# A hybrid encoder layer: level tiles in two sets, inverse blocks in four transfers, rotary halves exchanged by ScalarE

## The chip, the cores and the metric

The kernel runs on one core of a Trainium2 chip. The metric is the device time of one execution in microseconds (us), the median of several runs. Times inside an execution are read from a profile of one run, counted from the start of its span.

## What is computed

One layer of a bidirectional encoder over 1024 tokens of width 1024, in float32. Cut to what matters here:

```python
h = rms_norm(x, g_mix_pre)
proj = h @ w_in                      # attention q, k, v; delta q, k, v; gate; decay and beta
aq, ak = rope(aq), rope(ak)          # rotary positions, head width 64, halves of 32
attn_o = window_attention(aq, ak, av, sink)      # +-128 tokens, 8 heads on 2 key heads
dn_o = gated_deltanet(dqkv, gate, alpha, beta)   # 4 heads, two directions, chunked
x = x + rms_norm(concat(attn_o, dn_o) @ w_out)
x = x + rms_norm(cross_attention(rms_norm(x), rms_norm(mem)))
x = x + rms_norm(swiglu(rms_norm(x)))

def rope(x):                         # x1, x2 are the two halves of 32 of a head
    return concat([x1 * cos - x2 * sin, x2 * cos + x1 * sin])
# deltanet, per chunk: solve (I + strictly lower part) u = rhs, then a scan over the chunks
```

The reference works in chunks of 64 tokens. The kernel works in chunks of 128, for both directions, and inverts the triangular matrix of each chunk.

## The kernel before

The sequence lies in eight chunks of 128 tokens (NT = 8), feature rows on the partitions. Products are made in split precision: an operand is split into a high and a low part, and three products are summed (a projection of 128 columns is 24 matmuls of 128x512 for each half of 512 tokens, line 261). Weights come in by `load_w` (raw tile, then `whi` on ScalarE and `wlo` on VectorE). All transfers are issued by the SyncE queue, SP. The Tile framework puts the instructions of each engine in an order by priority (the order of the program) and a timing model, and adds the waits; each engine then works through its own list in that order. A tile's tag with `bufs=n` has n buffers; a new tile of that tag waits until one of them is free.

Three lists written by hand set the program's order. `ORDER_1` runs the projections of the delta heads (D), their preparation (P) and the base inverses of a pair of heads (B). `ORDER_2` is the part around the change:

```python
ORDER_2 = "L0 L1 G0 G1 A4 V A0 A1 L2 L3 W W W A2 A3 G2 G3 W".split()
```

L is `levels` of a delta head, G a gate projection, A an attention projection with rotary positions (A4 is the keys), V the value projection, W a pair of attention windows. `ORDER_3` then runs the scan of the delta heads (`s01`), which needs the result `d_pz` of all four heads, mixed with the remaining windows and with the cross-attention's keys and values.

**Levels.** `base_inverse` inverts all 32x32 diagonal blocks of a pair of heads by a chain of small VectorE products and stores them in DRAM (`d_inv`, lines 541 to 544). `levels(h)` builds from them the inverse of each 128x128 triangle, by two block products. It has large tiles `D5`, `D6`, `Z0`, `Z1` (128 x 8 x 128), zero off the diagonal blocks, in which the 32x32 blocks are placed at their diagonal position. Before the change there is one set of these (`wide_sets`, line 717), cleared once by POOL (line 719). The blocks come by twenty transfers for each head: for each of the four block rows `q` one to `m5`, one each into the diagonal place in `D5`, `D6`, `Z0`, `Z1` (`fetch`, line 551; each 32 x 8 x 32 numbers in runs of 128 bytes). A head is worked on in two halves of four chunks each (`part`), which alternate at each `yield`: load `Ul` (572), transpose (576), masks to `L5` and `L6` (577, 578), product with `L5` and `D5` (585, 591), small copies of the result `z5` to `D6`, `Z` and `mov6` (596 to 605), product with `L6` and `D6`, then `Z` to `d_pz` (610). `L5`, `L6` and `Ul` have two buffers each.

**Attention projection.** `attn_proj` multiplies each half of the product, in an accumulator bank of the pool `pg` (three banks), by the sine into `sn` and by the cosine into `rop`; four transfers for each half exchange blocks of 32 partitions from `sn` to `rot` (line 734); VectorE adds `rot` (735), ScalarE and VectorE split the sum into `qhi` and `qlo`, and both are stored. `sinT` carries the sign of the source row. `sn` shares its tag `rot` with `vT` of the value projection (line 745). Windows load the stored queries (`qs`, line 625).

Of the kernel before, what the change touches and what calls it, by code (L numbers as in the profile page):

```python
# [10 lines left out]
F32 = mybir.dt.float32  # L11
F32R = mybir.dt.float32r
I32 = mybir.dt.int32
AF = mybir.ActivationFunctionType
ALU = mybir.AluOpType
# [4 lines left out]
P = 128  # L20
# [12 lines left out]

ORDER_1 = "D0 P0 D1 P1 D2 B0 P2 D3 P3 B1".split()
ORDER_2 = "L0 L1 G0 G1 A4 V A0 A1 L2 L3 W W W A2 A3 G2 G3 W".split()
ORDER_3 = ("M " + "s01 W K " * 5 + "s01 K " * 3 + "s01 V V").split()
# [8 lines left out]
def host_constants():  # L47
    i = np.arange(P)
    blk = i // 32
    a, b = i[:, None], i[None, :]  # L50
    ba, bb = blk[:, None], blk[None, :]
    tri = {
        "ident": a == b,
        "mU": a < b,
        "mL": a > b,
        "mUi": a <= b,
        "mLi": a >= b,
        "m5": (ba // 2 == bb // 2) & (ba != bb),
        "m6": ba // 2 != bb // 2,
        "ones": a + b >= 0,  # L60
    }
    out = np.zeros((P, _NCONST), np.float32)
    for n, m in tri.items():
        out[:, _AT[n]:_AT[n] + P] = m

    out[:, _AT["band0"]:_AT["band0"] + P] = np.where(b >= a, 0.0, NEG)
    out[:, _AT["band2"]:_AT["band2"] + P] = np.where(b <= a, 0.0, NEG)
    half = np.arange(32, dtype=np.float32)
    inv = np.power(np.float32(10000.0), -half / np.float32(32)).astype(np.float32)
    out[:, _ROPE_AT] = inv[i % 32]  # L70
    out[:, _ROPE_AT + 1] = np.where(i % 64 < 32, 1.0, -1.0)
    return out


# [1 line left out]
def tile_hybrid_block(  # L76
# [469 lines left out]
    def levels(h):  # L546

        g, hh = h // 2, h % 2

        def fetch(dst, q, i, d):  # L550
            nc.sync.dma_start(dst, d_inv[g][i][d, hh, :, q].rearrange("c r s -> r c s"))

        m5 = tl_.tile([P, NT, 32], F32, tag="m5", name="m5", bufs=1)
        D5a, D6a, *Za = wide_sets[0]
        for q in range(4):
            r = slice(32 * q, 32 * q + 32)
            fetch(m5[r], q, 1, 1 - q % 2)
            fetch(D5a[r, :, r], q, 0, q % 2)
            fetch(D6a[r, :, r], q, 0, q // 2)
            for d in range(2):  # L560
                fetch(Za[d][r, :, r], q, 1, d)

        def part(b):
            c4 = slice(4 * b, 4 * b + 4)

            def wide(name):
                return tl_.tile([P, 4, P], F32, tag=name, name=name, bufs=2)

            L5, L6 = wide("L5"), wide("L6")
            D5, D6, Z = D5a[:, c4], D6a[:, c4], [z[:, c4] for z in Za]  # L570
            Ul = wide("Ul")
            nc.sync.dma_start(Ul, d_u[g][hh, c4].rearrange("c p n -> p c n"))
            yield
            p_ = small().rearrange("p (c n) -> p c n", c=4)
            for j in range(4):
                nc.tensor.transpose(p_[:, j, :], Ul[:, j, :], ident)
            nc.vector.tensor_tensor(L5, p_, bc(cm["m5"], 1, (P, 4, P)), ALU.mult)
            nc.vector.tensor_tensor(L6, p_, bc(cm["m6"], 1, (P, 4, P)), ALU.mult)

            def pair(lt, mv, dd, w):  # L580

                yield
                p_ = small()[:, 0:4 * w].rearrange("p (c n) -> p c n", c=4)
                for c in range(4):
                    nc.tensor.matmul(p_[:, c, :], lt[:, c, :], mv[:, c, :], start=True, stop=True)
                bs = tl_.tile([P, 4, 64], F32, tag="bs", name="bs", bufs=2)[:, :, 0:w]
                nc.scalar.copy(bs, p_)
                yield
                p_ = small()[:, 0:4 * w].rearrange("p (c n) -> p c n", c=4)
                for c in range(4):  # L590
                    nc.tensor.matmul(p_[:, c, :], dd[:, c, :], bs[:, c, :], start=True, stop=True)
                return p_

            p_ = yield from pair(L5, m5[:, c4, :], D5, 32)
            z5 = tl_.tile([P, 4, 32], F32, tag="z5", name="z5", bufs=2)
            nc.scalar.mul(z5, p_, -1.0)
            nc.vector.transpose(D6[32:64, :, 0:32], z5[0:32])
            nc.vector.transpose(D6[64:96, :, 96:128], z5[96:128])
            nc.vector.tensor_copy(Z[1][32:64, :, 0:32], z5[32:64])
            nc.vector.tensor_copy(Z[0][64:96, :, 96:128], z5[64:96])  # L600
            mov6 = tl_.tile([P, 4, 64], F32, tag="mov6", name="mov6", bufs=2)
            nc.scalar.copy(mov6[0:64], Z[1][0:64, :, 0:64])
            nc.vector.tensor_copy(mov6[64:128], Z[0][64:128, :, 64:128])
            nc.scalar.copy(Z[0][0:32, :, 32:64], z5[0:32])
            nc.scalar.copy(Z[1][96:128, :, 64:96], z5[96:128])
            p_ = yield from pair(L6, mov6, D6, 64)
            nc.scalar.mul(Z[0][0:64, :, 64:128], p_[0:64], -1.0)
            nc.vector.tensor_scalar(Z[1][64:128, :, 0:64], p_[64:128], -1.0, None, ALU.mult)
            for d in range(2):
                nc.sync.dma_start(d_pz[g][d][c4, :, hh, 1].rearrange("c p n -> p c n"), Z[d])  # L610

        together([part(b) for b in range(2)])
# [60 lines left out]
    keys, vhl = {}, None  # L673

    def window_keys(g):
        keys[g] = tw.tile([P, S], F32R, tag="khi", name="khi"), tw.tile([P, S], F32R, tag="klo", name="klo", bufs=1)
        for kk, src in zip(keys[g], d_k):
            for r in range(2):
                nc.sync.dma_start(f32(kk[64 * r:64 * r + 64]), src[64 * g:64 * g + 64, :])
# [32 lines left out]
    ps = pgs.enter_context(pool("psl", 2, space=PSUM))  # L712
    tw = p12.enter_context(pool("tw", 2))
    tw.tile([P, 384], F32, tag="sc", name="sc", bufs=8)
    vhl = tw.tile([P, NT + 1, 2, 2, 64], F32R, tag="vhl", name="vhl", bufs=1)[:, 0:NT]
    tl_ = p1.enter_context(pool("tl", 2))
    wide_sets = [[tl_.tile([P, NT, P], F32, tag=f"{n}{i}", name=n, bufs=1) for n in ("D5", "D6", "Z0", "Z1")] for i in range(1)]
    for t in wide_sets[0]:
        nc.gpsimd.memset(t, 0.0)

    def attn_proj(ct):
        pp = proj(w_in[:, ct * P:(ct + 1) * P])
        dst = [t[ct * P:(ct + 1) * P, :] if ct < 4 else t for t in (d_q if ct < 4 else d_k)]
        for hf in range(2):
            sl = slice(hf * HALF, (hf + 1) * HALF)
            rop = trp.tile([P, HALF], F32, tag="rop", name="rop")
            sn = trp.tile([P, HALF], F32, tag="rot", name="sn")
            rot = trp.tile([P, HALF], F32, tag="rot2", name="rot2")
            nc.vector.tensor_tensor(sn, pp[hf], sinT[:, sl], ALU.mult)
            nc.vector.tensor_tensor(rop, pp[hf], cosT[:, sl], ALU.mult)  # L730

            for q in range(4):
                o = 32 * (q ^ 1)
                nc.sync.dma_start(rot[32 * q:32 * q + 32], sn[o:o + 32])
            nc.vector.tensor_tensor(rop, rop, rot, ALU.add)
            hl = [trp.tile([P, HALF], F32R, tag=t, name=t) for t in ("qhi", "qlo")]
            split(*hl, rop)
            for t, o in zip(hl, dst):
                nc.sync.dma_start(o[:, sl], f32(t))
# [785 lines left out]
```

## Time and profile before

| | us |
|---|---|
| median of three runs | 1551.69 |
| lowest and highest | 1547.02, 1553.25 |
| profiled execution | 1555.78 |
| its span, first to last instruction | 1554.1 |
| mean granted TensorE clock | 0.983 |
| stretch of the levels and attention projections | about 221 to 373 |

The profiled execution is one run; its span is shorter than its time by 1.7 us, which lie around the instructions. In the rows, PE is TensorE (PEld its weight loads), DVE VectorE, ACT ScalarE, POOL GpSimd, SPq the queue of SyncE. The view by stretches gives the busy time of each engine in a part of the span, its number of instructions in brackets, the granted TensorE clock as a share of full speed, the mean busy share of the 16 DMA engines and their GB/s. A row of a tile's or a line's view gives, in ns, the shortest, the median and the longest of its instructions, then the start of the first and the last. A row of the waits gives who waited for whom, in us in all, how often, and the longest. A row of the chain gives the start, the length and what it was.

### The profile page before, as it was taken

What the parts mean: (1) busy time and instruction counts of PE and PEld (TensorE: products, weight loads), DVE (VectorE), ACT (ScalarE), POOL (GpSimd) and SP (SyncE); (2) the same over time, 40 slices, a digit from 0 to 9 for tenths busy, and PEclk for the clock granted to TensorE, in tenths of its full rate; (3) what the DMA queues carried; (4) which work ended last, traced back from release to release, by engine and by line L of the source; (5) the groups of instructions that cost most, each with busy time, mean ns of one, the idle gap of its engine ahead of it and who ended that gap; (6) DMA issues with size and microseconds to landing.
All of it is one profiled execution on the core that took longest, in us unless ns stands there. A gap on an engine that the chain in (4) does not pass through costs nothing.

```text
span 1554.1 us, 20931 instructions
## 1 busy us (share of the span) xinstructions
PE 1497.3 (96%) x7451; PEld 1258.1 (81%) x7451; DVE 1055.9 (68%) x1750; ACT 719.6 (46%) x1380; POOL 308.3 (20%) x305
## 2 busy tenths in 40 slices
PE   6999999898899999999999999999999999999998
PEld 5888888787899877888888777888888888888786
DVE  6777898766898766443447367776867554687665
ACT  6666552246556755454335574332323332454532
POOL 2000110000003201163102221433533333000021
PEclk9999999997999999999999999999999999999999
DMA  6244456867987584354213264344434334863354
GB/s 211 69 136 128 125 157 160 217 179 245 319 278 247 164 283 165 119 190 148 82 55 123 85 200 141 111 135 129 134 122 132 102 102 141 288 193 102 108 175 165
DMA packets 267366, 247.16 MB, mean 159 GB/s; under 512 B 39016, under 2 KB 204797, under 8 KB 267261
## 3 DMA queue, kind: packets, MB, share of 16 engines
q1 hardware_dynamic: 267261, 245.82, 50.7%
q8 instruction: 59, 0.97, 0.3%
q14 instruction: 46, 0.38, 0.1%
HBM read 173.65 MB, written 69.50 MB: 156 GB/s over the span
## 4 chain that ended last, share of the span: by engine, by line
PE 80%; DVE 6%; DMA 6%; ACT 3%; issue 2%; SPq 2%; POOL 0%; DVEq 0%; POOLq 0%; ACTq 0%
PE pg L261 13%; PE pmg L1016 10%; PE pD L1196 8%; PE pE L1196 8%; PE pA L1196 6%; PE pcq L261 6%; PE pdX L1386 6%; PE pdA L1386 4%; PE pB L1196 4%; PE psc L785 2%; PE pdX L1479 2%; PE pdD L1386 2%; DMA wraw<-in_w_ckv_dram 2%; PE pcs L1102 1%; PE pco L1128 1%
## 5 line engine op out<-in xcount | busy, mean ns | idle before, releaser
L102 ACT CAST whi<-wraw 128x1024 fp32r<-128x1024 f32 x108 | 113.5, 1051 | 173.3 <-PE pg L261 36.0
L103 DVE TENSOR_TENSOR wlo<-wraw,whi 128x1024 fp32r<-128x1024 f32 x78 | 95.5, 1225 | 77.7 <-ACT whi L102 75.0
L261 PE MATMUL pg<-hhi,whi 128*128 128x512 f32 x352 | 140.8, 401 | 0.2 <-DVE rop L730 0.2
L261 PE MATMUL pg<-hhi,wlo 128*128 128x512 f32 x352 | 140.2, 399 | 0.0
L261 PE MATMUL pg<-hlo,whi 128*128 128x512 f32 x352 | 139.9, 398 | 0.0
L1016 PE MATMUL pmg<-whi,b 128*128 128x512 f32 x384 | 118.4, 394 | 0.4 <-ACT b L102 0.4
L1196 PE MATMUL pA<-s,whi 128*128 128x512 f32 x352 | 109.5, 392 | 1.4 <-ACT m L1213 1.4
L103 POOL TENSOR_TENSOR wlo<-wraw,whi 128x1024 fp32r<-128x1024 f32 x30 | 73.8, 2460 | 143.3 <-ACT whi L102 143.2
L1016 PEld LDWEIGHTS pmg<-whi,b 128*128 128x128 f32 x384 | 71.3, 188 | 15.2 <-ACT b L102 1.3
L261 PEld LDWEIGHTS pg<-hhi,whi 128*128 128x128 f32 x352 | 67.3, 192 | 14.0 <-DVE rop L730 0.7
L261 PEld LDWEIGHTS pg<-hlo,whi 128*128 128x128 f32 x352 | 67.2, 191 | 13.2
L261 PEld LDWEIGHTS pg<-hhi,wlo 128*128 128x128 f32 x352 | 67.2, 191 | 13.1
L1196 PEld LDWEIGHTS pA<-s,whi 128*128 128x128 f32 x352 | 65.3, 188 | 15.2 <-ACT m L1213 2.0
L1386 PE MATMUL pdX<-dhl,whi 128*128 128x512 f32 x264 | 76.1, 390 | 1.5 <-DVE zv L1441 0.8
L1016 PE MATMUL pmg<-wlo,b 128*128 128x512 f32 x192 | 71.5, 392 | 0.0
L1196 PE MATMUL pA<-s,wlo 128*128 128x512 f32 x176 | 68.7, 392 | 1.1 <-DVE wlo L103 1.1
L102 ACT CAST whi<-araw 128x1024 fp32r<-128x1024 f32 (+1 forms) x36 | 35.4, 984 | 69.9 <-PE pdX L1386 27.6
L1273 POOL TENSOR_TENSOR act<-act,up 128x512 f32<-128x512 f32 x33 | 50.1, 1519 | 89.1 <-DVE up L1272 53.1
L103 DVE TENSOR_TENSOR wlo<-araw,whi 128x1024 fp32r<-128x1024 f32 (+1 forms) x36 | 40.8, 1133 | 38.4 <-ACT whi L102 38.3
L286 DVE SCALAR_TENSOR_TENSOR acc<-cp,cols,acc 128x1024 f32<-128x1024 f32 x48 | 61.5, 1282 | 1.5 <-ACT acc L284 0.8
L1386 PEld LDWEIGHTS pdX<-dhl,whi 128*128 128x128 f32 x264 | 49.3, 188 | 12.8 <-issue 1.1
L1246 DVE TENSOR_TENSOR sr<-sr,wraw 128x512 f32<-128x512 f32 x22 | 37.8, 1716 | 29.8 <-POOL sr L1245 29.8
(409 smaller groups left out, 3976.7 us busy)
## 6 DMA issues: line engine op xcount, KB each, us to landing
wraw<-in_w_gate_up_dram SPq DMA_DIRECT2D x52, 512.0 KB, 4.0
kv<-d_kv SPq DMA_DIRECT2D x32, 512.0 KB, 6.6
wraw<-in_w_in_dram SPq DMA_DIRECT2D x22, 512.0 KB, 5.5
b<-in_w_down_dram SPq DMA_DIRECT2D x20, 512.0 KB, 6.8
araw<-d_as SPq DMA_DIRECT2D x20, 512.0 KB, 3.8
pz<-d_pz SPq DMA_DIRECT2D x32, 256.0 KB, 6.8
wraw<-in_w_ckv_dram SPq DMA_DIRECT2D x16, 512.0 KB, 6.4
wraw<-in_w_out_dram SPq DMA_DIRECT2D x16, 512.0 KB, 4.3
```

Of the source, the lines that this page charges most:

```text
L102: nc.scalar.copy(hi, src)
L103: (eng or nc.vector).tensor_tensor(lo, src, f32(hi), ALU.subtract)
L261: nc.tensor.matmul(p_, w[:, k, :], ah[a][:, k, :], start=(k == 0 and i == 0), stop=(k == nk - 1 and i == 2))
L286: nc.vector.scalar_tensor_tensor(acc, cp[:, t:t + S], taps[t], acc, ALU.mult, ALU.add)
L785: nc.tensor.matmul(out[:, d, h, :], lt[:, d, h, :], rt[:, d, h, :], start=True, stop=True)
L1016: nc.tensor.matmul(pp[t], act[a][:, k, tt], w_[:, kk, :], start=(k == 0 and i == 0), stop=(k == KT - 1 and i == 2))
L1102: nc.tensor.matmul(pp[:, t2_, :], q[a][:, ct, tt], kr_[b_][:, ct, :], start=(j == 0 and i == 0), stop=(j == 1 and i == 2))
L1196: nc.tensor.matmul(out_, w[a][:, k, :], xx[b_][:, k, :], start=(start and k == 0 and i == 0), stop=(k == HK - 1 and i == 2), skip_group_ch ...
L1246: nc.vector.tensor_tensor(s[1], s[0], a_[:, 0:HK], ALU.subtract)
L1273: nc.gpsimd.tensor_tensor(o_, o_, up, ALU.mult)
L1386: nc.tensor.matmul(banks[t], a[:, k - k0, tt], w, start=(first and k == 0 and i == 0), stop=(k == NB - 1 and i == 2), skip_group_check=not ...
L1479: nc.tensor.matmul(X[t], a[:, k], w[:, k0 + k], start=False, stop=(k0 + k == NB - 1 and i == 2), skip_group_check=True)
```

## The change

1. There are two sets of the large tiles; head `h` uses set `h % 2`. POOL clears both.
2. The inverse blocks of a head come in four transfers of 128 x 8 x 32 numbers into tiles `c` with three buffers. POOL copies them into `D5` and `D6` (eight copies), ScalarE into `m5`, `Z0` and `Z1` (twelve copies).
3. `L5`, `L6` and `Ul` share one tag with four buffers; `mov6` and `khi` have one buffer in place of two; `vhl` loses a spare chunk.
4. In `attn_proj` ScalarE copies the exchanged blocks of 32 partitions out of the accumulator into `rot`, VectorE multiplies by the cosine and, after the copies, by the sine; the sign in the constants is turned to that of the target row. `rot` and `qhi` share a tag with two buffers, as do `vT` and these.

```diff
+LT = 4
+LC = 3
...
-    out[:, _ROPE_AT + 1] = np.where(i % 64 < 32, 1.0, -1.0)
+    out[:, _ROPE_AT + 1] = np.where(i % 64 < 32, -1.0, 1.0)
...
-        def fetch(dst, q, i, d):
-            nc.sync.dma_start(dst, d_inv[g][i][d, hh, :, q].rearrange("c r s -> r c s"))
+        def fetch(i, d):
+            t = tl_.tile([P, NT, 32], F32, tag="c", name="c", bufs=LC)
+            nc.sync.dma_start(t, d_inv[g][i][d, hh].rearrange("c b r s -> (b r) c s"))
+            return t
 
         m5 = tl_.tile([P, NT, 32], F32, tag="m5", name="m5", bufs=1)
-        D5a, D6a, *Za = wide_sets[0]
+        D5a, D6a, *Za = wide_sets[h % 2]
+        cw = [fetch(0, d) for d in range(2)]
         for q in range(4):
             r = slice(32 * q, 32 * q + 32)
-            fetch(m5[r], q, 1, 1 - q % 2)
-            fetch(D5a[r, :, r], q, 0, q % 2)
-            fetch(D6a[r, :, r], q, 0, q // 2)
-            for d in range(2):
-                fetch(Za[d][r, :, r], q, 1, d)
+            nc.gpsimd.tensor_copy(D5a[r, :, r], cw[q % 2][r])
+            nc.gpsimd.tensor_copy(D6a[r, :, r], cw[q // 2][r])
+        cz = [fetch(1, d) for d in range(2)]
+        for q in range(4):
+            r = slice(32 * q, 32 * q + 32)
+            nc.scalar.copy(m5[r], cz[1 - q % 2][r])
+        for d in range(2):
+            for q in range(4):
+                r = slice(32 * q, 32 * q + 32)
+                nc.scalar.copy(Za[d][r, :, r], cz[d][r])
...
-                return tl_.tile([P, 4, P], F32, tag=name, name=name, bufs=2)
+                return tl_.tile([P, 4, P], F32, tag="L", name=name, bufs=LT)
...
-            mov6 = tl_.tile([P, 4, 64], F32, tag="mov6", name="mov6", bufs=2)
+            mov6 = tl_.tile([P, 4, 64], F32, tag="mov6", name="mov6", bufs=1)
...
-        keys[g] = tw.tile([P, S], F32R, tag="khi", name="khi"), tw.tile([P, S], F32R, tag="klo", name="klo", bufs=1)
+        keys[g] = tw.tile([P, S], F32R, tag="khi", name="khi", bufs=1), tw.tile([P, S], F32R, tag="klo", name="klo", bufs=1)
...
-    vhl = tw.tile([P, NT + 1, 2, 2, 64], F32R, tag="vhl", name="vhl", bufs=1)[:, 0:NT]
+    vhl = tw.tile([P, NT, 2, 2, 64], F32R, tag="vhl", name="vhl", bufs=1)
...
-    wide_sets = [[... for n in ("D5", "D6", "Z0", "Z1")] for i in range(1)]
-    for t in wide_sets[0]:
+    wide_sets = [[... for n in ("D5", "D6", "Z0", "Z1")] for i in range(2)]
+    for t in wide_sets[0] + wide_sets[1]:
         nc.gpsimd.memset(t, 0.0)
...
             rop = trp.tile([P, HALF], F32, tag="rop", name="rop")
-            sn = trp.tile([P, HALF], F32, tag="rot", name="sn")
-            rot = trp.tile([P, HALF], F32, tag="rot2", name="rot2")
-            nc.vector.tensor_tensor(sn, pp[hf], sinT[:, sl], ALU.mult)
-            nc.vector.tensor_tensor(rop, pp[hf], cosT[:, sl], ALU.mult)
-
+            rot = trp.tile([P, HALF], F32, tag="rot", name="rot")
             for q in range(4):
                 o = 32 * (q ^ 1)
-                nc.sync.dma_start(rot[32 * q:32 * q + 32], sn[o:o + 32])
+                nc.scalar.copy(rot[32 * q:32 * q + 32], pp[hf][o:o + 32])
+            nc.vector.tensor_tensor(rop, pp[hf], cosT[:, sl], ALU.mult)
+            nc.vector.tensor_tensor(rot, rot, sinT[:, sl], ALU.mult)
             nc.vector.tensor_tensor(rop, rop, rot, ALU.add)
-            hl = [trp.tile([P, HALF], F32R, tag=t, name=t) for t in ("qhi", "qlo")]
+            hl = [trp.tile([P, HALF], F32R, tag=t, name=n) for t, n in (("rot", "qhi"), ("rot2", "qlo"))]
```

More of the change, by code (lines that the diff above doesn't have):

```diff
@@ L714, in tile_hybrid_block @@
     tw.tile([P, 384], F32, tag="sc", name="sc", bufs=8)
-    vhl = tw.tile([P, NT + 1, 2, 2, 64], F32R, tag="vhl", name="vhl", bufs=1)[:, 0:NT]
+    vhl = tw.tile([P, NT, 2, 2, 64], F32R, tag="vhl", name="vhl", bufs=1)
     tl_ = p1.enter_context(pool("tl", 2))
-    wide_sets = [[tl_.tile([P, NT, P], F32, tag=f"{n}{i}", name=n, bufs=1) for n in ("D5", "D6", "Z0", "Z1")] for i in range(1)]
-    for t in wide_sets[0]:
+    wide_sets = [[tl_.tile([P, NT, P], F32, tag=f"{n}{i}", name=n, bufs=1) for n in ("D5", "D6", "Z0", "Z1")] for i in range(2)]
+    for t in wide_sets[0] + wide_sets[1]:
         nc.gpsimd.memset(t, 0.0)
```

## The prediction

> **What bounds the kernel now.** I read the page first, then the stretches around the change, then TensorE's waits, the chain, and single tiles. Figures are microseconds from the span's start.
>
> ```profile
> span 1554.1 us, 20931 instructions
> PE 1497.3 (96%) x7451; PEld 1258.1 (81%) x7451; DVE 1055.9 (68%) x1750; ACT 719.6 (46%) x1380; POOL 308.3 (20%) x305
> ```
>
> TensorE sets the time: the other engines can lose work or gain it without moving the end, unless TensorE comes to wait or stops waiting. The edited lines (`levels`, `attn_proj`) run between 221 and 373, so what the change can win is what TensorE loses there. The view by stretches gives it:
>
> ```profile
> core 0: us, PE busy (x) PEld busy (x) DVE busy (x) ACT busy (x) POOL busy (x), PEclk, DMA share, GB/s
> 235.00:362.00 127.00, 119.81 (x644) 102.75 (x643) 92.08 (x212) 45.35 (x108) 3.40 (x5) 0.95 0.73 192
> 254.00:264.00 10.00, 8.20 (x28) 6.91 (x29) 8.41 (x22) 4.93 (x13) 0.00 (x0) 0.66 0.50 122
> 295.00:320.00 25.00, 20.07 (x98) 16.72 (x98) 12.79 (x29) 6.05 (x12) 0.00 (x0) 0.86 0.86 211
> 320.00:360.00 40.00, 39.77 (x238) 34.89 (x236) 28.07 (x73) 23.19 (x59) 0.99 (x3) 1.00 0.75 210
> 360.00:385.00 25.00, 21.07 (x102) 17.76 (x102) 14.80 (x41) 15.17 (x38) 2.15 (x5) 0.66 0.63 205
> 385.00:410.00 25.00, 21.12 (x135) 18.76 (x134) 20.38 (x54) 15.37 (x38) 0.40 (x2) 0.86 1.00 335
> ```
>
> I count as lost: length minus PE busy, plus PE busy times (1 - PEclk), since matmuls run longer while the clock is held down. 254 to 264: 1.80 + 8.20 x 0.34 = 4.6. 295 to 320: 4.93 + 20.07 x 0.14 = 7.7. 360 to 385: 3.93 + 21.07 x 0.34 = 11.1. 385 to 410: 3.88 + 21.12 x 0.14 = 6.8. From 320 to 360 only 0.2 is lost. In all 30 us, 1.9% of the span: a ceiling. What TensorE waited for in these stretches, and the chain there:
>
> ```profile
> PE psw L633 <- DMA qs<-d_q: 3.9, 1, 3.9
> PE ptv L749 <- ACT vT L746: 2.0, 1, 2.0
> ...
> PE pow L664 <- ACT ph L102: 2.0, 1, 2.0
> PE ps L585 <- ACT vhl L102: 1.1, 1, 1.1
> ...
> 253.03 2.03 DMA rot<-sn
> ...
> 276.66 4.43 DMA d_pz<-Z
> 281.16 0.51 SPq L551
> ...
> 305.53 0.63 SPq L625
> 306.21 5.30 DMA qs<-d_q
> ...
> 359.89 2.87 DMA Z<-d_inv
> ```
>
> The reader is to see three things. At 253 the rotary exchange is a DMA; `vT` shares a tag with its source, so ScalarE and then TensorE wait for it (2.0 us idle, and the clock stays down until 264). At 305 a window's query load is only issued after a long run of other issues by the one queue, SP; TensorE idles 3.9. At 360 the levels of the last head still wait for their inverse blocks; the scan cannot begin without them.
>
> **The change, part by part.** *Inverse blocks and rotary exchange leave SP.*
>
> ```profile
> L551 SPq DMA_DIRECT2D D<-d_inv x32: 390/452/874, 239.4 to 352.3; - x32
> L551 SPq DMA_DIRECT2D Z<-d_inv x32: 302/449/1042, 240.4 to 359.9; - x32
> L551 SPq DMA_DIRECT2D m<-d_inv x16: 320/467/1333, 238.6 to 325.6; - x16
> L734 SPq DMA_DIRECT2D rot<-sn x40: 507/588/1240, 251.1 to 340.6; - x40
> L739 SPq DMA_DIRECT2D d_q<-qhi x8: 326/478/1531, 272.6 to 347.9; - x8
> DMA to landing us min/median/max: 2.2/2.6/5.6
> ```
>
> (The last row is of the tile `qhi`.) Eighty fetches of about 0.45 are 36 us of SP's time and forty exchanges of 0.588 are 23.5: 60 us of the 121 from 238.6 to 359.9. Sixteen larger fetches come back. Their issue is not in the trace; between 0.45 (an issue like today's) and 1.33 (the longest of these rows) they cost 7 to 21 us; I take 0.5, as the 256 KB stores of `qhi` issue in 0.478, so 8. SP is relieved by about 50 us, and everything behind it (query loads, weight loads, `d_pz` stores) issues earlier.
>
> *Copies that take their place.*
>
> ```profile
> L746 ACT COPY vT<-pg x2: 586/586/586, 255.2 to 257.4; 128x512 f32<-128x512 f32 x2
> L602 ACT COPY mov<-Z x8: 406/407/408, 258.9 to 363.9; 64x256 f32<-64x256 f32 x8
> 241.26 2.26 POOL L528 TENSOR_SCALAR_AFFINE_SELECT A<-A 128x1024 f32<-128x1024 f32 x1 [16.94 <-DVE A L527]
> L719 POOL MEMSET D<- x2: 947/948/950, 212.8 to 213.7; 128x1024 f32 x2
> ```
>
> ScalarE gets 40 copies of 512 elements from PSUM (0.586 by the `vT` row: 23.4 us) and 48 of 256 elements in SBUF (0.407 by the `mov` row: 19.5 us): 43 us onto 45.35 busy of 127, so it goes from 36% to 70%. It is not the bound, but each instruction queued there waits longer. Behind ScalarE's queue stand the `whi` casts of the next projection, `ph` and the small copies of the level chain; `vT`, `ph` and `vhl` on ScalarE cost TensorE 2.0 + 2.0 + 1.1 = 5.1 in the rows above, of which `vT` is the rotary DMA. The other 3.1, doubled with the load on ScalarE, is 3 us of new waiting; the bounds are 0 and 10 (a quarter of the added work on TensorE's path). POOL gets 32 copies of 256 elements, which the trace does not show: a fill of 1024 takes 0.948 and a select over 1024 took 2.26, so between 0.24 and 0.57 each, 8 to 18 us, on an engine that is busy 3.4 of 127; I take 0.5, as a copy reads and writes like the select, so 16. That is cover enough; if a copy is late, the first block product of that head is late by the eight copies, at most 4 us. Four more fills (3.8 us) stand before the first copies, at about 214, where POOL is idle. New is a wait on SP: a head's four transfers share three `c` buffers, so the fourth stands in SP's queue until POOL has emptied the first, at most those 4 us; the weight and query loads queued behind it are late by as much, 16 us over four heads against the 50 that SP is relieved of, so 0 in the sum.
>
> *VectorE* keeps three passes per rotary half in another order, at the same price (0.69 by the `pm` row below, of the same size). What can touch it is POOL:
>
> ```profile
> 242.31 1.74 DVE L496 TENSOR_TENSOR pm<-pc,C 128x512 f32<-128x512 f32 x1
> L496 DVE TENSOR_TENSOR pm<-pc,C x16: 681/690/1735, 99.7 to 242.3; 128x512 f32<-128x512 f32 x16
> ```
>
> The one `pm` that ran beside POOL's select (241.26 to 243.52) took 1.735 against a median of 0.690: it ended half a microsecond after the select. So 16 us of POOL copies can push VectorE by as much, of 35 us that it idles in the 127; half of it falls on the base inverse's chain of small products and moves heads 2 and 3 by up to 8 us. I take none of it for the sum, as those heads gain more than that below. The Trainium skill says the same as these rows in "SBUF — State Buffer", section "SBUF: two separate sides": VectorE with two SBUF inputs and a GpSimd op that reads SBUF lock each other out for a whole instruction. By that rule the copies are not free beside the inverse; the sum would be about 4 us poorer if half of the lock-outs reached TensorE.
>
> *Two sets of level tiles.* Today head 1 cannot fetch until head 0's blocks are stored (276.66 + 4.43, then SP's L551 at 281.16), and so on from head to head.
>
> ```profile
> 295.37 1.29 SPq L543 DMA_DIRECT2D d_inv<-A  x2
> 320.36 0.94 SPq L572 DMA_DIRECT2D Ul<-d_u  x2
> 349.30 1.45 SPq L610 DMA_DIRECT2D d_pz<-Z  x2
> ...
> 322.22 1.70 PE ps L585 x16
> ...
> 337.77 0.84 PE ps L585 x8
> ...
> L610 SPq DMA_DIRECT2D d_pz<-Z x16: 360/536/1442, 271.3 to 373.4; - x16
> L261 PE MATMUL pg<-hhi,wlo x25: 387/393/478, 331.4 to 358.6; 128*128 128x512 f32 x25
> L793 SPq DMA_DIRECT2D kv<-d_kv x8: 319/376/709, 374.7 to 386.6; - x8
> ```
>
> The blocks of heads 2 and 3 are on their way at 296.7. Head 2's first block product starts at 322.2 and its last stores issue at 349.3, 27 us later; head 3 ends at 373.4 and the scan's first load goes out at 374.7, though the last projection was over at 358.6. After: store and fetch some 3 each (2.6 in the `qhi` row), eight POOL copies 4, so the first product of head 2 at about 308, its stores at 335, and head 3, half a chain behind (one `m5` buffer, four `L` buffers), at about 349. That lies before the end of the projections, so the scan would start when those end.
>
> *The sum.* 254 to 264: the DMA that caused it is gone, 4.6. 295 to 320: the query load no longer queues behind SP, but its own 5.3 us of flight and the `vhl` wait stay possible; I take 5.5 of 7.7. 360 to 385: the levels are no longer last; next late are the scan's own loads and the windows' short chains (`ph`, `pl`), so half, 5.5 of 11.1. 385 to 410: the DMA engines are full (share 1.00) with scan and weight loads, which the change does not touch: 0. Gains 15.6, less 3 of new waits on ScalarE: 12.6, say 12. The profiled execution took 1555.78 (span 1554.1 and 1.7 around it), so 1543.8 there; it lies 4.1 over the median of 1551.69, and in terms of that median I forecast 1540.
>
> A rule of the Trainium skill bears on the first term: "TensorE: Matmul & The Clock Gate", section "Why this matters for your kernels", holds the clock safe for gaps up to about 3 us. The trace does not agree, with 2.03 us idle and the clock at 0.66 until 264. By the rule only the idle 1.8 would come back there, and the sum would be 9, not 12.
>
> **Rivals.** *The level chain stays serial.* Each half of a head needs three `L` tiles, and there are four for all. If the second half's load must wait until the first half's second block product has released a tile, a half holds the ring from its load at 320.36 to 337.77, 17.4 us; four halves after 297 end at 367, and with the 11.5 from second product to last store at 378, no earlier than the 373 of now. Against it: a loaded `Ul` is free again after four transposes, so the tiles may pass on much sooner; no view of this kernel shows which way the slots go. Then the third term stays away and 4.6 + 5.5 - 3 = 7 remain: 1545.
>
> *Slower: the rotary ring holds the accumulators.* `rot` and `qhi` now share two buffers, and a projection's bank is free only when four ScalarE copies have found one. A half needs a buffer for four copies and two passes, 4 x 0.586 + 2 x 0.69 = 3.7, then again for the cast (0.59, as `vT`), the issue 0.48 and the flight 2.6, 3.7: 7.4 in two buffers, one half per 3.7. A half costs TensorE 24 matmuls:
>
> ```profile
> 228.38 21.36 PE pg L261 x94
> ```
>
> 0.227 each, 5.45 per half. It turns at 10.9 us of buffer time per half. Flights of 5.6 occur, and ScalarE at 70% makes every copy and cast queue; at 15 us, one half per 7.5 and ten halves, TensorE loses 20 us, and 12 gained leaves 8 lost: 1560. For it: the longest flight in the row above; against it: gate and value projections stand between the rotary ones, and SP, which delays those stores now, has half its load.
>
> **How the numbers follow.** Half a per cent, 7.8 us, is about what a measurement of this kernel can tell from no change (the three runs spread over 6.2). Forecast 0.52; serial levels 0.26; rotary ring 0.22. The forecast's own range: 1528 if all three stretches (23.4) come back, 1546 if ScalarE takes 10. It is faster by over 0.5% in 0.43 of its 0.52, the serial case in 0.05, so 0.48. Slower: 0.19 from the ring and 0.04 from a serial case whose POOL copies also reach the inverse, 0.23. Within: 0.29. The range goes from 1526 (a little of the last stretch too) to 1560.
>
> **What would show it.** Right: no TensorE wait for `vT` near 253, the clock 1.00 from 254 to 264; `d_pz` stores done by about 350 and the first scan load near the last projection; PE busy from 350 to 375 above 23 of 25. Wrong: stores of `Z` still near 370 (serial levels); matmuls into `pg` waiting for DVE or ACT at lines of `attn_proj` (ring); ScalarE releasing most of TensorE's idle time; or the loss after 385 growing by what was won before it.

## The result and the profile after

The changed kernel takes 1562.95 us in the median (1560.78 to 1565.37, six runs), the kernel before 1551.03 (1547.02 to 1553.25, six runs): a ratio of 1.0082, with a 95% interval of 1.0067 to 1.0096. It is slower by 12 us; the forecast was 1540, and the range ended at 1560.

The profiled execution of the kernel before, at 1555.78, lay 5 us above its median. A second profile of the same kernel (experiment f1) took 1549.56 with a span of 1547.8, so the readings below set the profile after (1562.19, span 1560.4) against that one. First the page after. TensorE has the same 7451 products; they keep it busy for 1496.9 us, where it was 1490.6 in the second profile before and 1497.3 in the first.

```profile
span 1560.4 us, 20960 instructions
PE 1496.9 (96%) x7451; PEld 1256.8 (81%) x7451; DVE 1060.8 (68%) x1750; ACT 760.8 (49%) x1468; POOL 326.5 (21%) x341
```

The view by stretches (columns as in the prediction), the kernel before in its second profile:

```profile
250.00:300.00 50.00, 48.00 (x257) 40.92 (x255) 42.77 (x98) 14.03 (x35) 0.16 (x1) 0.93 0.73 195
300.00:350.00 50.00, 43.89 (x245) 37.89 (x245) 30.56 (x76) 20.76 (x52) 0.79 (x2) 0.97 0.73 191
350.00:375.00 25.00, 21.56 (x140) 18.60 (x138) 15.08 (x45) 17.68 (x44) 0.40 (x2) 0.99 0.77 211
375.00:400.00 25.00, 21.31 (x130) 18.20 (x131) 21.29 (x54) 16.74 (x41) 2.35 (x6) 0.87 1.08 346
400.00:450.00 50.00, 48.47 (x389) 46.38 (x388) 46.59 (x130) 24.80 (x60) 0.60 (x3) 1.00 1.04 318
450.00:600.00 150.00, 142.38 (x875) 125.53 (x874) 110.60 (x247) 99.03 (x241) 25.08 (x33) 0.97 0.69 224
```

and the kernel after:

```profile
250.00:300.00 50.00, 48.45 (x249) 40.67 (x250) 44.67 (x94) 33.92 (x70) 8.68 (x18) 0.97 0.54 148
300.00:350.00 50.00, 45.02 (x244) 39.08 (x243) 26.76 (x71) 35.30 (x81) 7.07 (x18) 0.90 0.72 188
350.00:375.00 25.00, 19.53 (x112) 17.39 (x111) 14.78 (x47) 14.36 (x44) 0.40 (x2) 0.80 0.29 77
375.00:400.00 25.00, 19.64 (x102) 16.94 (x103) 18.41 (x48) 13.81 (x35) 2.20 (x5) 0.80 0.67 218
400.00:450.00 50.00, 45.27 (x350) 42.67 (x349) 43.83 (x120) 26.67 (x66) 0.80 (x4) 0.97 1.08 316
450.00:600.00 150.00, 141.14 (x919) 124.83 (x919) 116.41 (x266) 98.45 (x239) 26.48 (x33) 0.99 0.76 250
```

So of the 12.6 us between the two spans half (6.3) is busy time and half is idle time; the busy half is the same work done more slowly. Lost time by the prediction's rule (idle, plus busy time by what the clock was short) counts both. Row by row, before to after: 5.4 to 3.0, 7.4 to 9.5, 3.7 to 9.4, 6.5 to 9.3, 1.5 to 6.1, 11.9 to 10.3. The first row wins 2.4, the stall of the rotary transfer; the four after it lose 15.2; in all +11.2 of the 12.6 between the spans. From 350 to 400 the DMA engines have little to do (0.29 and 0.67 where it was 0.77 and 1.08): the scan's loads are not out yet. Why, the rows of single lines show. The kernel before (second profile): last store of `Z`, last product of the projections, the scan's first product:

```profile
L610 SPq DMA_DIRECT2D d_pz<-Z x16: 377/550/1082, 272.9 to 371.6; - x16
L261 PE MATMUL pg<-hhi,wlo x352: 387/389/628, 25.2 to 359.8; 128*128 128x512 f32 x176
L785 PE MATMUL psc<-kv,pz x128: 270/275/421, 380.6 to 509.7; 128*128 128x128 f32 x128
```

and the same three lines after, with two rows of the chain that ended last:

```profile
L620 SPq DMA_DIRECT2D d_pz<-Z x16: 359/370/801, 289.5 to 385.4; - x16
L263 PE MATMUL pg<-hhi,wlo x352: 387/389/774, 24.5 to 346.9; 128*128 128x512 f32 x176
L793 PE MATMUL psc<-kv,pz x128: 270/275/551, 394.0 to 526.3; 128*128 128x128 f32 x128
...
385.40 3.45 DMA d_pz<-Z
388.93 4.93 DMA pz<-d_pz
```

The projections end 12.9 us earlier, as was forecast. The levels end 13.8 us later, the scan starts 13.4 later, and the span is 12.6 longer. So a delay as long as the whole loss is there when the scan starts.

### The profile page after: what moved, and what is told of

Same layout as the page of the kernel before. It is cut to its first block, busy times and chain, and to the rows that moved or that the text cites. A ratio compares the mean times of both kernels' runs of the same rounds, so it can differ in the third digit from the quotient of the medians.

```text
span 1560.4 us, 20960 instructions
## 1 busy us (share of the span) xinstructions
PE 1496.9 (96%) x7451; PEld 1256.8 (81%) x7451; DVE 1060.8 (68%) x1750; ACT 760.8 (49%) x1468; POOL 326.5 (21%) x341
## 4 chain that ended last, share of the span: by engine, by line
PE 65%; DVE 4%; DMA 4%; ACT 3%; issue 1%; SPq 0%; POOL 0%; DVEq 0%; POOLq 0%; ACTq 0%
PE pmg L1024 11%; PE pE L1204 8%; PE pD L1204 8%; PE pA L1204 6%; PE pcq L263 6%; PE pdX L1394 6%; PE pdA L1394 4%; PE pB L1204 4%; PE psc L793 3%; PE pdD L1394 2%; PE pcs L1110 1%; PE pco L1136 1%; PE pdX L1487 1%; PE pck L924 1%; PE psw L643 1%
## 5 line engine op out<-in xcount | busy, mean ns | idle before, releaser
L263 PEld LDWEIGHTS pg<-hhi,wlo 128*128 128x128 f32 x352 | 67.1, 191 | 13.4
```

What stands on the lines that cost most here:

```text
L263: nc.tensor.matmul(p_, w[:, k, :], ah[a][:, k, :], start=(k == 0 and i == 0), stop=(k == nk - 1 and i == 2))
```

## The experiments

In the table the ratio is to the kernel before on the same chip; the three times are from the profile of each: the issue of the last store of `Z`, the scan's first product with `pz`, and the span.

| run | what it is | ratio (95%) | last store | scan | span |
|---|---|---|---|---|---|
| f1 | before, again | 0.9998 (0.9987 to 1.0009) | 371.6 | 380.6 | 1547.8 |
| f4 | before + rotary edit, own tags | 0.9961 (0.9947 to 0.9976) | 365.8 | 373.4 | 1544.9 |
| e1 | before + rotary edit, shared tags | 1.0043 (1.0026 to 1.0060) | 369.8 | 375.3 | 1552.5 |
| f3 | before, four L buffers | 1.0030 (1.0018 to 1.0042) | 380.8 | 387.8 | 1555.4 |
| f2 | before, one `mov6` | 1.0073 (1.0056 to 1.0089) | 382.5 | 391.9 | 1558.4 |
| e2 | before, both rings | 1.0089 (1.0069 to 1.0108) | 385.2 | 393.9 | 1560.8 |
| g1 | f4 + block transfers, one set | 1.0004 (0.9987 to 1.0021) | 371.9 | 381.4 | 1547.1 |
| g2 | g1, all copies on POOL | 1.0086 (1.0062 to 1.0109) | 389.0 | 395.7 | 1561.0 |
| h3 | f4, `khi` and `vhl` cut | 1.0102 (1.0080 to 1.0125) | 376.1 | 384.9 | 1559.3 |
| h2 | h3 + second pair of `Z` | 1.0097 (1.0075 to 1.0120) | 377.7 | 387.4 | 1563.3 |
| k1 | h3 + 5 KB unused | 0.9990 (0.9973 to 1.0008) | 364.0 | 371.4 | 1546.9 |
| after | | 1.0082 (1.0067 to 1.0096) | 385.4 | 394.0 | 1560.4 |
| e3 | after, all copies on POOL | 1.0061 (1.0046 to 1.0076) | 383.0 | 391.7 | 1556.5 |
| e4 | after, one set, full rings | 1.0044 (1.0026 to 1.0063) | 381.7 | 387.7 | 1558.1 |
| g3 | after, one set | 1.0090 (1.0065 to 1.0115) | 391.5 | 400.8 | 1565.5 |
| g4 | after, own rotary tags | 1.0072 (1.0046 to 1.0097) | 385.5 | 393.0 | 1561.9 |
| h1 | after, two `mov6` | 1.0105 (1.0082 to 1.0127) | 379.1 | 387.9 | 1558.2 |
| k2 | after, `c` in another pool | 1.0332 (1.0287 to 1.0376) | 414.8 | 423.4 | 1596.0 |
| k3 | k2, two `mov6` | 1.0305 (1.0275 to 1.0335) | 418.1 | 426.1 | 1597.6 |

Over all of them the last store moves by 54 us, from 364.0 to 418.1, while what follows it (span less last store) stays between 1172 and 1186. The kernel is as long as the chain of `levels` plus a constant, though only to within 14 us, which is as much as the loss itself: a late chain explains the large differences in the table, not those of a few us. (h1 and h3 were profiled in their shortest runs, 5 us below their medians, and their spans are short by that; the other profiles lie within 4 us of their medians.)

**The kernel before, again (f1).**

> The kernel before, unchanged: a second profile of it. If the profile shown at first was an ordinary execution, its milestones repeat within 1 us (projections' last product 358.6, last store of Z 373.4, first scan product 382.8, first pmg 569.7, last pmg 902.0, span 1554.1), and the rotary edit alone, with its earlier milestones (375.3, 562.8, 897.3) but a median of +0.43%, lost its time behind the last pmg. If that profile was 4 to 6 us slow, as its own time of 1555.78 against the median of 1551 says, the new one shows where: first pmg near 563 to 565 and a span near 1549.

It was the second: 1549.36, with the last store of `Z` at 371.6 and a span of 1547.8. So the milestones of e1, which looked early beside the first profile, are those of an ordinary execution up to the scan. At the end of the output projection's products e1 is 0.7 us later than f1 (897.3 and 896.6), at the end of the span 4.7: most of its loss against the kernel before lies behind 900, and no run says why. In f4 and k1 that last part is as long (655 us), in f1 and g1 it takes 651 and 652.

**The two rings of the levels alone (e2).** On the kernel before:

```diff
-return tl_.tile([P, 4, P], F32, tag=name, name=name, bufs=2)
+return tl_.tile([P, 4, P], F32, tag="L", name=name, bufs=4)
-mov6 = tl_.tile([P, 4, 64], F32, tag="mov6", name="mov6", bufs=2)
+mov6 = tl_.tile([P, 4, 64], F32, tag="mov6", name="mov6", bufs=1)
```

> The kernel before with the rings cut alone: L5, L6 and Ul share four buffers, mov6 has one. Ring theory: head times grow from about 24 us as in the changed kernel, the last d_pz store goes from 373 to 383 or later, ratio 1.005 to 1.010. ScalarE theory: no copy is added, the first halves and second halves shift a few us, last d_pz store below 377, ratio 0.998 to 1.003.

1562.48: the loss of the whole change, with nothing else of it. The two parts by themselves:

> The kernel before with one mov6 buffer in place of two, all else as it was. If the single mov6 (one half of a head waits for the other's) makes the loss of the rings: +0.5 to +0.9%, heads of 30 us and more, last store of Z near 384. If the four buffers shared by L5, L6 and Ul make it: within 0.2% of before, heads of 25 us.

> The kernel before with L5, L6 and Ul in one tag of four buffers in place of three tags of two, mov6 in two. If the four buffers make the loss: +0.5 to +0.9%, Ul of a head transposed only after the head before has finished with its L6, last store of Z near 384. If the single mov6 makes it: within 0.2%, last store near 373. If each costs half, both runs come out at +0.3 to +0.5%.

One `mov6` costs 0.73%, four L buffers 0.30%, both together 0.89%. Neither price is one of waits alone, since Tile orders the instructions anew: in f1 the two halves' first products of head 1 start at 282.85 and 287.42 with products of the projections between them, in f3 they stand together at 283.88, and from about 254 (in f2 from about 265) to 585 the order on TensorE, VectorE and ScalarE is another. The products with `mov6` show what one buffer does. In head 0 nothing is lost yet (the second half's product starts at 270.11 before and at 269.75 in f2). Those of head 1, in the timeline of TensorE, before (second profile), then f2:

```profile
298.58 1.00 PE L585 MATMUL ps<-mov,L 128*128 128x64 f32 x8
301.04 1.08 PE L585 MATMUL ps<-mov,L 128*128 128x64 f32 x8 [0.93 <-ACT vhl L102]
```

```profile
298.21 1.08 PE L585 MATMUL ps<-mov,L 128*128 128x64 f32 x8 [1.74 <-DVE mov L603]
306.23 1.00 PE L585 MATMUL ps<-mov,L 128*128 128x64 f32 x8
```

The two halves are 2.5 us apart before and 8.0 in f2 (in head 2, 1.3 and 8.8). The second half's copies into `mov6` come after the first half's product, and its own product has a later place in TensorE's list. In the kernel after (SP's, POOL's and TensorE's timelines) the same step in head 0, and the next heads:

```profile
275.78 1.08 PE L595 MATMUL ps<-mov,L 128*128 128x64 f32 x8 [1.45 <-ACT qhi L104]
285.41 1.00 PE L595 MATMUL ps<-mov,L 128*128 128x64 f32 x8
...
307.97 0.40 POOL L563 COPY D<-c 32x256 f32<-32x256 f32 x1
308.81 0.55 SPq L582 DMA_DIRECT2D Ul<-d_u  x1
...
334.84 1.00 PE L601 MATMUL ps<-bs,D 128*128 128x64 f32 x8
336.31 0.60 PE L586 MATMUL ps<-ident,Ul 128*128 128x128 f32 x4
...
342.95 0.98 PE L595 MATMUL ps<-m,L 128*128 128x32 f32 x8
```

The halves of head 0 are 9.6 apart, and the ring is not all of that: the first half's product is over at 276.86, but ScalarE's copy into `mov6` starts at 283.57, behind rotary copies, a cast of `whi` and one of `qhi` in its list. Head 2 has its blocks in its own set of `D` tiles by 308.4 and its `Ul` is loaded at 308.8, but it is transposed at 336.3, after the last product of head 1 at 334.8. The second set is filled early and its `D` tiles stand ready for 28 us. Four L buffers for tiles of which each half needs three fit this order of things; that the rings hold the heads, and not the sets, rests on f3, e2 and g3. ScalarE's list holds them as well. Its rows while head 1 is worked on, in the kernel after:

```profile
306.35 1.64 ACT L571 COPY Z<-c 32x256 f32<-32x256 f32 x4 [3.19 <-DMA c<-d_inv]
308.01 0.27 ACT L597 COPY bs<-ps 128x128 f32<-128x128 f32 x1
...
316.22 1.75 ACT L740 COPY rot<-pg 32x512 f32<-32x512 f32 x3 [5.05 <-DMA d_q<-qhi]
317.98 0.30 ACT L614 COPY Z<-z 32x128 f32<-32x128 f32 x1
```

Block copies for head 2 stand in front of head 1's small copies `bs`, and ScalarE waits 3.2 us for their transfer; rotary copies stand in front of head 1's copies of `z`, and ScalarE waits 5.0 for a store of `qhi`. Head 1 takes 43 us from its transposes to its last product (292.0 to 334.8), where f1 takes 29 (276.7 to 305.9).

**The second set (g3, h2).** g3 is the kernel after with `wide_sets[h % 2]` put back to `wide_sets[0]` and one set cleared:

> The kernel after with one set of level tiles in place of two, its four L buffers and single mov6 kept. If the second set frees the heads from each other: slower than after by 3 us and more (1566 and above). If the four L buffers already keep the heads one after another, the second set has nothing to free: within 2 us of 1563. Against the run with one set and full rings (1556.4) the difference is the price of the two rings in this company: by the runs on the kernel before, 10 to 13 us.

1564.78 against 1562.95: the second set brings 2 us or nothing under these rings. h2 gives a second pair of `Z0` and `Z1` to the kernel of the rotary edit, with the rings whole; room for it comes from `khi` and `vhl`, and h3 is its control.

```diff
-keys[g] = tw.tile([P, S], F32R, tag="khi", name="khi"), ...
+keys[g] = tw.tile([P, S], F32R, tag="khi", name="khi", bufs=1), ...
-vhl = tw.tile([P, NT + 1, 2, 2, 64], ...)[:, 0:NT]
+vhl = tw.tile([P, NT, 2, 2, 64], ...)
```

> The kernel of the rotary edit with its own tags (1544.3), blocks by direct transfers, rings whole, with a second pair of Z0 and Z1 (D5 and D6 stay single), khi in one buffer and vhl without its spare chunk. By the prediction's step for two sets (head 3 half a chain behind head 2): last store at 350 to 358 instead of 365.8, time 1530 to 1538. If D5, D6, m5 and the base inverses of the second pair of heads set when a head can begin: last store within 2 us of the control's, time within 0.2% of it.

> The control for h2: the kernel of the rotary edit with its own tags, khi in one buffer and vhl without its spare chunk, one set of level tiles. If these two cuts cost nothing: 1543 to 1546 (0.996 of before). If the keys of the second pair of windows must wait for khi: 1547 to 1552, a longer wait of windows' first product on a DMA of khi or klo.

The second pair brings nothing (1.0097 against 1.0102): but for two more clears on POOL, the instructions of TensorE, VectorE, ScalarE and POOL stand in the order of h3. `D5`, `D6` and `m5` are single in h2, so what two full sets do with whole rings is not shown by any run. The surprise is the control: two cuts that were to be free cost 1.4% of f4.

**Where the level tiles lie (k1).** An unused tile of 5 KB for each partition takes the place of what h3 cut; `khi` stays single.

```diff
+tw.tile([P, 1280], F32, tag="pad", name="pad", bufs=1)
```

> The kernel of h3 (rotary edit with own tags, khi in one buffer, vhl without its spare chunk) with an unused tile of 5 KB for each partition in the windows' pool, so that the pool of the level tiles starts where it did. If the place of the level tiles makes h3's loss: level tiles cleared near 214 us, first block product near 252, time 1543 to 1547 (0.996 to 0.998 of before). If the single khi makes it: cleared near 214 too, but time still 1556 and above. Half and half: 1550 to 1554.

1548.46 against 1566.55 (0.9990 and 1.0102 of before), and up to 428 us the instructions of k1 stand in the order of f4 again. So the loss of h3 is not the single `khi` (that leaves about 4 us, the distance of k1 to f4) but the place of the pool of level tiles, which the cuts move 5 KB down. The rows of POOL's clearing, of `Ul`'s loads and of the first block product, h3 and then k1:

```profile
L719 POOL MEMSET D<- x2: 951/952/952, 243.7 to 244.6; 128x1024 f32 x2
L572 SPq DMA_DIRECT2D Ul<-d_u x8: 392/447/593, 253.4 to 337.8; - x8
L585 PE MATMUL ps<-m,L x64: 190/276/276, 265.3 to 363.5; 128*128 128x32 f32 x64
```

```profile
L720 POOL MEMSET D<- x2: 949/950/951, 212.7 to 213.6; 128x1024 f32 x2
L572 SPq DMA_DIRECT2D Ul<-d_u x8: 377/400/757, 217.8 to 321.4; - x8
L585 PE MATMUL ps<-m,L x64: 190/276/401, 250.7 to 351.3; 128*128 128x32 f32 x64
```

In k1 the tiles are first used at 213, in h3 at 243. In POOL's list the clearing of h3 stands behind a step of the base inverse, which waits 17.4 us for VectorE and ends where the clearing starts. That the cuts move the pool onto memory of tiles of the stage before, which come free later, is the likely reason for this order; which tiles they are was not traced. The kernel after has the same two cuts, and the same rows:

```profile
L729 POOL MEMSET D<- x4: 946/952/954, 243.4 to 247.9; 128x1024 f32 x4
L582 SPq DMA_DIRECT2D Ul<-d_u x8: 359/528/797, 246.3 to 348.4; - x8
L595 PE MATMUL ps<-m,L x64: 190/276/276, 256.4 to 370.2; 128*128 128x32 f32 x64
```

**Lifting the place in the kernel after (k2, k3): not settled.** The `c` tiles were taken from the windows' pool (`tw.tile` for `tl_.tile`), so that the level tiles lie 3 KB higher.

> The kernel after with the c tiles taken from the windows' pool, which lies in front of the pool of the level tiles: the same memory in all, the level tiles 3 KB higher, all rings as in the kernel after. If the place of the level tiles holds the kernel after: tiles cleared near 214 us, first block product near 250, last store of Z before 380, time 1550 to 1557. If the four L buffers and the single mov6 hold it wherever the tiles lie (the rings alone gave 1562.5 on the kernel before, with the tiles cleared at 213): 1560 to 1564.

> As k2, with two mov6 buffers and two c buffers. If both the place and the single mov6 hold the kernel after, each hiding the other: 1545 to 1552, last store of Z before 374. If the place alone does: as k2. If neither: 1560 and above.

Both missed by 35 us and more. The level tiles are cleared at 213.9, but now the first load into a `c` tile is issued at 296.8, where it was 242.8 in the kernel after; the likely reason, again, is memory that comes free late:

```profile
L554 SPq DMA_DIRECT2D c<-d_inv x16: 360/494/3829, 296.8 to 369.9; - x16
L595 PE MATMUL ps<-m,L x64: 191/276/402, 313.5 to 397.6; 128*128 128x32 f32 x64
```

They fit the reading that a tile's place decides when it is first used, and they leave open how much of the loss of the kernel after its place makes.

**The rotary edit alone (f4, e1).** f4 has ScalarE's copies on the kernel before, with `qhi` and `qlo` in tags of their own; e1 has them share `rot` and `rot2`, as in the kernel after.

> The kernel before with the rotary halves copied by ScalarE, qhi and qlo in tags of their own as before (in the run of the rotary edit alone they shared rot and rot2). If the shared buffers cost the +0.43% of that run: within 0.2% of before. If the copies on ScalarE themselves cost it: +0.3 to +0.5% again. My theory of the prediction (stall at 254 us gone, ScalarE's copies nearly free) says -0.3%.

> The kernel before with the rotary edit alone (ScalarE copies, shared buffers of rot and qhi). Ring theory (the level chain is late because four L buffers and one mov6 buffer make heads and halves follow each other): nothing of that is in here, SP loses 23 us of issues, the projections end near 347 as after the whole change, the last d_pz store at or before 373; 1540 to 1547, ratio 0.993 to 0.998. ScalarE theory (the level chain's small steps stand behind the new copies in ScalarE's list): 23.4 of the 43 us of copies are in here, so about half of the 12 us of delay; last d_pz store near 379, ratio 1.000 to 1.005.

f4 gains 0.39%, e1 loses 0.43%: the shared tags cost 0.8%, more than the edit brings. In the view of stretches for the windows' score tile `psw`, 375 to 450, f4 and then e1:

```profile
375.00:450.00 75.00, 10.97 (x42) 7.48 (x42) 11.40 (x21) 0.98 1.02 320
```

```profile
375.00:450.00 75.00, 7.57 (x32) 5.44 (x32) 9.00 (x17) 0.98 1.06 335
```

The scans of the two start within 2 us; in e1 fewer of the windows' products run beside the scan (32 for 42), the last of them comes at 548 in place of 537, and TensorE waits 10.5 us for the windows' short chains in place of 6.2 (`ph` and `pl` together). Against that, the windows' score products wait less (1.4 for 5.6), so this is not all of the 7.6 us between the two spans: 3.4 of them are there when the output projection starts (559.4 and 562.8), and 3.4 more are one wait of TensorE for VectorE at 588, which k1 has too, without shared tags. How the shared tags bring about that order was not followed further. In the kernel after, where the scan waits for the levels anyhow, own tags change nothing:

> The kernel after with qhi and qlo in tags of their own, one buffer each, and rot in its two (the same memory as in the kernel after). If sharing rot with qhi costs what it cost on the kernel before (0.7%, 1554.9 against 1544.3): 1552 to 1556. If the rings of the levels hide it, because the scan waits for the levels anyhow: 1560 to 1563. If one buffer each for qhi and qlo is a worse ring: above 1563.

1562.29 for 1562.95.

**The block transfers and their copies (g1, g2, e3).**

> The kernel of the rotary edit with its own tags (0.9961 of before, 1544.3 us) plus the four block transfers with their copies on POOL and ScalarE, one set of level tiles, every ring as it was before. If the transfers and copies are worth something in themselves: below 1544, near 1538 (0.992), with head 3's last store before 362. If ScalarE's 48 block copies stand in front of the small copies of the level chain: 1548 to 1552, heads longer than 25 us, idle time before products of the levels that ends with ScalarE.

> As g1, with all twenty block copies of a head on POOL. If ScalarE's queue is what the copies cost: 3 to 6 us less than g1, as in the same swap made on the kernel after. If POOL's copies hold VectorE or are themselves too long a chain (20 x 0.4 = 8 us for each head): equal to g1 or slower.

> The changed kernel with the twelve block copies of a head moved from ScalarE to POOL (19.5 us off ScalarE, twenty copies of 0.4 = 8 us a head on POOL). ScalarE theory: the wait of head 0's z and mov steps shrinks by about half, last d_pz store from 385 to near 376 to 380, ratio to the kernel before 1.000 to 1.005. Ring theory: heads still follow each other strictly, last d_pz store 383 or later, ratio 1.006 to 1.010.

With everything else kept, four transfers and twenty copies for each head are slower than twenty transfers: g1 takes 1549.6 against 1544.3 for f4, and the last store comes at 371.9 for 365.8. With all copies on POOL the same kernel loses 14.6 more (g2), where the kernel after wins 4.4 from that swap (e3; 0.2% by the ratios). In the kernel after, ScalarE's queue is longer than POOL's and the second set lets POOL copy ahead; in g2 the twenty copies stand between a head's blocks and its first product. Whether that is all of the difference in sign was not tested.

**Undoing rings in the kernel after (e4, h1).**

> The changed kernel with one set of large tiles, which makes room for six L buffers and two of mov6; transfers, ScalarE copies and rotary edit stay. Ring theory: a head's time goes back to about 25 us, last d_pz store 373 or earlier, ratio 0.993 to 1.000. ScalarE theory: a head still takes over 35 us in heads 0 and 1, and with one set the heads cannot overlap at all, last d_pz store 385 or later, ratio 1.006 to 1.015.

> The kernel after with two mov6 buffers (and two c buffers in place of three, to make room). If the single mov6 holds the level chain of the kernel after: last store of Z 5 to 8 us earlier than 385.4, time 1554 to 1557. If the four L buffers alone keep the heads apart there: last store within 2 us of 385, time 1560 to 1564.

e4 takes 1556.36, half of the loss; against g3, its price of the two rings in this company is 8.4 us. h1, with the second `mov6` (and one `c` buffer less), is at 1564.67 no faster, though its profile has the last store 6 us earlier.

## Why the prediction was wrong, by its steps

**What bounds the kernel.** "TensorE sets the time" was read from the busy share, and the 30 us lost were taken as stretches that can each be won. The stretch was the right one, but what sets the end is the chain of `levels`, since the scan can start no earlier. In f1 its last store came 12 us after the last projection, and the change lengthened that to 38.5 (385.4 less 346.9).

**254 to 264, 4.6 won: right there, but not around it.** After the change TensorE is busy for all 10.00 us there at a clock of 1.00; of the 50 us from 250, though, only 2.4 are won: about 3 are lost in the rest of them, where it was about 1. The clock rule of the Trainium skill that the prediction weighed ("TensorE: Matmul & The Clock Gate", section "Why this matters for your kernels": gaps up to about 3 us safe) does not hold in f4 either. Stretches of it:

```profile
250.00:254.00 4.00, 2.65 (x19) 2.14 (x17) 3.74 (x10) 0.41 (x2) 0.00 (x0) 1.00 0.42 68
254.00:264.00 10.00, 10.00 (x51) 8.64 (x51) 8.77 (x23) 4.22 (x12) 0.00 (x0) 0.83 0.95 272
...
300.00:350.00 50.00, 48.48 (x277) 42.52 (x276) 29.64 (x77) 31.86 (x72) 0.61 (x3) 0.97 0.77 202
```

The first two: 1.35 us idle, then 10 us without a gap at 0.83.

**295 to 320, 5.5 won: near for the rotary edit, lost in the whole.** f4 loses 3.0 from 300 to 350 (the last row above), where f1 loses 7.4, so 4.4 are won. In the kernel after that stretch loses 9.5.

**360 to 385, 5.5 won: the step that failed.** The prediction had head 2's first product at 308 and head 3's stores at 349. Measured: 342.95 and 385.4, beyond even the 370 that the text named as the sign of serial levels. It took the two sets as what separates the heads and granted "half a chain behind" for the rings. The rings turned out to cost 0.3% (the L buffers) and 0.7% (`mov6`) by themselves. `mov6` with one buffer was named in the change and given no price.

**POOL's clears "at about 214, where POOL is idle": failed.** They ran at 243.4, behind a step of the base inverse that ended then. Nothing in the step asked which memory the tiles lie on; the sizes of `khi` and `vhl` were named in the change and given no price either. k1 shows that the place of the tiles can cost 17 to 18 us.

**ScalarE's 43 us of copies, 3 us: too small, and at another place.** The durations held. The groups of copies (busy time, mean ns; then the idle time before them and what ended it) and a row of TensorE's waits, after:

```profile
L740 ACT COPY rot<-pg 32x512 f32<-32x512 f32 x40 | 23.1, 578 | 8.3 <-DMA d_q<-qhi 5.0 <-PE pg L263 2.7
L571 ACT COPY Z<-c 32x256 f32<-32x256 f32 x32 | 12.9, 402 | 4.3 <-DMA c<-d_inv 3.2 <-DMA d_pz<-Z 0.7
PE pow L674 <- ACT ph L104: 8.4, 9, 2.6
```

TensorE's wait for `ph` rose from 3.6 in f1 to 8.4. What the price left out is the level chain: with copies on both engines it ends 6 us later in g1 than in f4. The prediction named the small copies of that chain as standing behind ScalarE's queue, but priced only the waits of TensorE; in the kernel after those copies come late, by the rows of ScalarE's list above.

**POOL's copies at 0.5: within the bounds of 0.24 to 0.57** (medians of 0.399, up to 0.857, in 16 each). **VectorE beside them, 0 in the sum: right.** One of the inverse's steps while POOL copies, after:

```profile
250.68 0.45 DVE L538 TENSOR_TENSOR A<-A,tmpb 128x184 f32<-128x184 f32 x1
```

The same step took 0.35 in f1, so 0.1 us more, and the next two steps lose about as much each (0.44 for 0.37, 0.45 for 0.38).

**The rivals.** The serial level chain was the right mechanism. Its price was not: 378 for the last store was taken as hardly later than before, with the other gains kept, and the case came out at 1545. It also held L5, L6 and `Ul` alone to be the ring. The rotary ring was right that sharing `rot` with `qhi` is dear (0.8% in e1 against f4), and in the kernel after ScalarE does wait 5.0 us with its copies for a store of `qhi`, in front of the level chain. But it named the accumulators, and the projections end early in both (346.3 in e1, 346.9 after); and in the kernel after, own tags win nothing (g4).

**What adds up.** Alone, the rings cost 0.9% on the kernel before and the place of the tiles 1.1% and more on f4 (k1 to h3); the block copies cost 0.4% on f4, and the rotary edit brings 0.4%. The whole is +0.8%. The three losses (rings, place, block copies) all delay the same chain, and inside the kernel after, with one thing lifted, the rest still holds it: a second `mov6` wins nothing (h1), nor do own rotary tags (g4), the block copies taken off ScalarE win 4 us (e3), and whole rings in place of the second set win half of the loss (e4). How the 12 us divide among them inside the kernel after stays open.

The best kernel of the study is f4, the rotary edit with its own tags and nothing else: 1544.3 us, 0.9961 (0.9947 to 0.9976) of before.

## What to carry to other kernels

When a change buys a second buffer set with memory from other tiles, give each ring that it shortens a price on the chain that uses it; here the set brought nothing that a run could show, and the shortened rings alone, on the kernel before, cost as much as the whole change. A busy engine is not yet the bound: find the one event that the next stage waits for, and see whether an edit moves that. Copies that take the place of transfers stand in an engine's list, and what waits for them there can be another chain: ask which small copies come behind. And a tile that grows or shrinks moves the pools behind it, so look when the moved tiles are first used.

## What the runs showed of the hardware

A ScalarE copy of 32 partitions by 512 from PSUM takes 0.578 us, as long as one of 128 partitions (0.586 in the prediction's row of `vT`), so moving four blocks of 32 cost four full copies here. POOL's copy of 32 by 256 takes 0.399, hardly other than ScalarE's 0.402 (median and mean, kernel after). In f4 one wait of 1.35 us was followed by 10 us without a gap in which the granted clock was 0.83.
